# Gate column sums of the second layer as steps of the attention flow, and the last residual on one engine

## The chip, the cores and the metric

One core of a Trainium2 chip runs the whole program. The metric is device time in microseconds; 793.57 us is the median of three runs of the kernel before (793.48 to 795.55). The engines are named as in the profile: PE (matrix products), DVE (vector), ACT (scalar), POOL (GpSimd), and SP, which only issues transfers. Each engine works through its own list of instructions in a fixed order; where an instruction waits, all behind it on that engine wait too.

## The reference

Two layers work on 512 latent tokens and 256 context tokens of width 1024. Layer 0 is differential attention, layer 1 grouped-query attention with 8 query heads and 2 key heads. Both have the same frame:

```
shift, scale, gate = split(silu(c) @ ada_w[i] + ada_b[i])
h = rms_norm(x, pre_g[i]) * (1 + scale) + shift
y = (attention(h) * silu(z)) @ w_out[i]
x = x + gate * rms_norm(y, post_g[i])
```

The change concerns two pieces of layer 1: the gate, a row of 1024 numbers made from silu(c) and a 1024 x 1024 part of `ada_w[1]`, and the last line, which adds the gated, normalised product to the residual x. In layer 1 only the latent tokens are kept.

## The kernel before

**Numbers and stages.** All products are done in three matmuls on split operands (a high part, and the rest), `mm3`, whose recorder has line 155. The order of the stages is: layer 0 up to about 445 us of the trace; its output product, the residual and the transposed input of layer 1; the keys and values of layer 1 (K and V); then layer 1's attention from about 575 us, with the remaining query projections (`q_proj`) and gate-path projections (`z1_proj`) as filling; last the output product, tile by tile of 128 tokens, and the store of `out`.

**The planner.** The attention of a layer is traced by `flow` (L366). It holds streams of `Step`s, each with a cost in microseconds of a planner's clock and a due time: its own `at`, and lags behind other steps. The step that is due first is traced; while none is due, `piece` (L331) traces one more piece of the projections in `fillq` and moves the clock on by its cost. In layer 1 a score unit (S_, L1527) is a quarter of a head's tokens: six score matmuls, a maximum on DVE (L1537), an exponential on ACT (L1543), a reciprocal on DVE (L1544), the scaling of the weights on POOL (L1545, recorded in L233). There are 32, `TS/2` = 4.52 us of clock apart at the soonest, and each at least `SLAG1` behind the one two before. T_ steps transpose the weights and split them into `ah` (ACT, L1561) and `al` (DVE, L1562); M_ steps multiply them with the values (L167), at least `LM[layer]` behind their transposes. X_ steps transpose queries, Y_ steps finish the gate. `LM[0]` is the lag in layer 0 and `LM[1]` that in layer 1.

**Order on the engines.** Steps marked hot are traced at a raised priority (`HOT0`, `HOT1`, one number for each stream); the builder then places each engine's instructions by priority, as soon as what they need is there. An instruction may so stand well ahead of its place in the code: the first two gate loads are issued at 554.9 us, while values are still being projected. `tc.issue_after(ins)` ties instructions behind `ins` on the same engine.

**The gate.** `gate1_part` (L1585) is called eight times right after `q_proj(0)`, before any other filling. Each call loads 512 KB of `ada_w[1]` from SP into one of two buffers `gw`, and DVE multiplies each of its two 128 x 512 halves with a column of silu(c) and adds it to `gate1` (L1596 for the first of a half, else L1598). `gate1_finish` (L1600) sums `gate1` over the partitions with two matmuls, adds `ada_b` and multiplies by `post_g`; its two calls come at units 10 and 13 (`GFIN`).

**A bank and its readers.** The four PSUM banks of projections and transposes are handed round. A bank of `q_proj` is free again when ACT has squared it (L1408) and DVE has formed the two rope products `ta` (L1397) and `tb` (L1399, two instructions; `tb` has one buffer, which POOL empties in L1402).

**The end.** For each token tile the last columns of the output product are squared and summed on ACT (L1672), gated on DVE (L1688), and with the reciprocal root r (for the last tile L424 and L425 on ACT) the residual is formed in two pieces of 512 on DVE (L1703). For the last tile they are three: 512 columns on DVE, 256 as a scaling on ACT (L1700) and a sum on POOL (L1701), and 256 on DVE. Each piece is stored, the middle one from ACT, the others from SP (L1704).

Of the kernel before, what the change touches and what calls it, by code (L numbers as in the profile page):

```python
# [9 lines left out]
F32 = mybir.dt.float32  # L10
F32R = mybir.dt.float32r
AF = mybir.ActivationFunctionType
ALU = mybir.AluOpType
# [3 lines left out]
P = 128  # L17
# [16 lines left out]
ACD = 0.54  # L34
FILL1 = (('q', 1), ('z', 0), ('z', 2), ('q', 2), ('z', 1), ('q', 3), ('z', 4), ('z', 5), ('z', 3), ('z', 6), ('z', 7))
HOT0 = (4682, 2421, 950, 3759)
HOT1 = (1476, 3151, 2600, 3663, 2938)
WARM = 1817
AGB = 10
PRE = 16.26  # L40
# [13 lines left out]
LT = (1.27, 1.44)  # L54
AHEAD = 2
SLAG = (4.74, 1.08)
SLAG1 = 5.1
AT1 = 12.82
EGL = 'v'
EXS = 'pvvvvv'  # L60
# [15 lines left out]
EG1 = 'a'  # L76
EGA = "v"
RL = 3.57
LM = (4.78, 5.5)
AB = 3  # L80


# [5 lines left out]
def tile_backbone(  # L88
# [23 lines left out]
    nc = tc.nc  # L112
    uid = [0]

    def nm(s):
        uid[0] += 1
        return f"{s}_{uid[0]}"
# [8 lines left out]
    def small(n=1):  # L126
        return sm.tile([P, 8], F32, tag="sm", name=nm("sm"), bufs=24)[:, :n]
# [10 lines left out]
    def pj(n):  # L138
        i = lru.pop(0)
        o = banks[i][:, :n]  # L140
        held[id(o)] = (o, i)
        return o
# [62 lines left out]
    scol = con.tile([P, 2, KT], F32, name="scol")  # L205
# [29 lines left out]
    VP = {"v": nc.vector, "p": nc.gpsimd}  # L235
# [56 lines left out]
    def get_wout(layer, c, n):  # L292
        return [ws.get(k) for k in wout_keys(layer, c, n)]
# [18 lines left out]
    @contextmanager  # L312
    def onward(prev):
        if prev is None:
            yield
        else:
            with tc.issue_after(prev.ins), tc.high_priority(offset=20000):
                yield

    def hot(f, *args):  # L320
        with tc.high_priority(offset=HOT):
            f(*args)
# [8 lines left out]
    def piece():  # L331
        i = 0
        while i < min(len(fillq), AHEAD):
            try:
                cost = next(fillq[i])
            except StopIteration:
                fillq.pop(i)
                continue
            if cost is None:
                i += 1  # L340
                continue
            clock[0] += cost
            return True
        return False

    def drain(gen=None):
        while fillq and (gen is None or gen in fillq):
            ok_ = piece()
            assert ok_ or not fillq or (gen is not None and gen not in fillq)
# [16 lines left out]
    def flow(layer, streams):  # L366
        streams = [list(q) for q in streams]
        while any(streams):
            if layer == 0:
                rope_due()  # L370
            due, i = min((q[0].due(), i) for i, q in enumerate(streams) if q)
            if due > clock[0] and piece():
                continue
            assert due < 1e8
            step = streams[i].pop(0)
            clock[0] = max(clock[0], due)
            if step.hot:
                with tc.high_priority(offset=(HOT0, HOT1)[layer][i]):
                    step.f()
            else:  # L380
                step.f()
            clock[0] += step.cost
            step.t = clock[0]

    def chunk(layer, tstep, mstep, kts, after, ts, ms):
        for i, kt in enumerate(kts):
# [3 lines left out]
            if len(ms) >= AB:  # L390
                t.lag.append((ms[-AB], 0.0))
            m = Step(lambda kt=kt: mstep(kt), 0.65, [(t, LM[layer])])
            ts.append(t)
# [34 lines left out]
    def run(gen):  # L428
        for _ in gen:
            pass  # L430

    def out_proj(o, ghi, glo, w, m, n, lo=0, hi=KT):
        sl = slice(m * P, (m + 1) * P)
        per = 1024 // n
        for kt in range(lo, hi):
            wh, wl = w[kt // per]
            c = slice((kt % per) * n, (kt % per) * n + n)
            mm3(o, ghi[kt][:, sl], glo[kt][:, sl], wh[:, c], wl[:, c], kt == 0, kt == KT - 1)
            yield 3 * n / 2400.0
# [373 lines left out]
    with tc.tile_pool(name="t0", bufs=1) as t0:  # L813
# [39 lines left out]
        def rope_due():  # L853
            while ropeq and ropeq[0][0] <= clock[0]:
                ropeq.pop(0)[1]()

        def last_of(eng):
            return next(i for i in reversed(nc.cur_bb.bb.instructions) if i.engine == eng.engine)

        def qk_split(*args):  # L860
            with tc.high_priority(offset=WARM):
# [30 lines left out]
        def qr_tile():  # L892
            return t0.tile([P, T], F32, tag="qr", name=nm("qr"), bufs=4)
# [256 lines left out]
        for which, o in enumerate((oq, ok)):  # L1150
            r = qr_tile()
# [24 lines left out]
        S_, T_, M_, X_ = [], [], [], []  # L1176
# [101 lines left out]
    x1 = [h1p.tile([P, D], F32, name=f"x1_{t}", bufs=1) for t in range(NQ)]  # L1278
    gate1 = h1p.tile([P, D], F32, name="gate1")
# [98 lines left out]
    with tc.tile_pool(name="t1", bufs=1, side="right") as t1p:  # L1378
# [81 lines left out]
        t1q = ctx.enter_context(tc.tile_pool(name="t1q", bufs=1))  # L1460
# [121 lines left out]

            chunk(1, tstep, mstep, (0, 2, 4), [after], ts, ms)

        def gate1_part(half, k2):  # L1585
            acc = gate1[:, half * 512:half * 512 + 512]
            gw = t1q.tile([P, 1024], F32, tag="gw", name=nm("gw"), bufs=2)
            nc.sync.dma_start(
                gw.rearrange("p (k n) -> p k n", k=2),
                ada_w[1, k2 * 256:(k2 + 1) * 256, 2 * D + half * 512:2 * D + half * 512 + 512].rearrange("(k p) n -> p k n", p=P),  # L1590
            )
            for k in range(2):
                kt = k2 * 2 + k
                gs = gw[:, k * 512:(k + 1) * 512]
                if kt == 0:
                    VP[EGA].tensor_scalar(acc, gs, scol[:, 0, kt:kt + 1], None, ALU.mult)  # L1596
                else:
                    VP[EGA].scalar_tensor_tensor(acc, gs, scol[:, 0, kt:kt + 1], acc, ALU.mult, ALU.add)  # L1598

        def gate1_finish(half):  # L1600
            acc = gate1[:, half * 512:half * 512 + 512]
            o = pj(512)
            colsum(o, acc, [t1q.tile([P, 512], F32R, tag=t, name=nm("ac"), bufs=n) for t, n in (("za", 1), ("sz", 2))])
            b = wp.tile([P, 1024], F32, tag="raw", name=nm("raw"), bufs=2)
            sl = slice(half * 512, half * 512 + 512)
            nc.sync.dma_start(b[:, :512], ada_b[1, 2 * D + half * 512:2 * D + half * 512 + 512].partition_broadcast(P))
            nc.sync.dma_start(b[:, 512:], post_g[1, sl].partition_broadcast(P))
            nc.vector.tensor_tensor(acc, o, b[:, :512], ALU.add)
            close(o)
            nc.vector.tensor_tensor(acc, acc, b[:, 512:], ALU.mult)  # L1610
# [12 lines left out]

        add(q_proj(0))
        drain()
        for i in range(8):
            gate1_part(i // 4, i % 4)
        for kind, i in fill1:
            add({"q": q_proj, "z": z1_proj}[kind](i))
        S_, T_, M_, X_ = [], [], [], []  # L1630
# [15 lines left out]
        for h in range(KT):  # L1646
# [4 lines left out]
            for ch in range(2):  # L1651
                at, u = s1_units(h, (2 * ch, 2 * ch + 1))
                for i, st_ in enumerate(u):
                    st_.at = at_ + TS * (h * 2 + ch + i / 2)
                    st_.lag.append((qtr[h], 2.5))
                    if len(S_) >= 2:
                        st_.lag.append((S_[-2], SLAG1))
                    if len(T_) >= 6:
# [3 lines left out]
                    T_.append(Step(tail1, 0.0, [(M_[-1], 0.0), (u[-1], 0.0)]))  # L1662
                pv1_steps(h, at, ch, u[-1], T_, M_)
        Y_ = [Step(lambda i=i: gate1_finish(i), 0.9, [(S_[GFIN[i]], 0.0)], hot=False) for i in range(2)]
        flow(1, [S_, T_, M_, X_, Y_])
        drain()
        w_o = w_o[0]
        u, ss = {}, {}
# [5 lines left out]
        for qi, (c, n) in enumerate(OUTC1):  # L1674
            w = get_wout(1, c, n) if qi else w_o
            if qi == 0:
                for m in range(NQ):
                    run(out_proj(o_pre[m], ghi, glo, w, m, n, KT - 1, KT))
            for m in range(NQ):
                o = pj(n) if qi else o_pre[m]  # L1680
                if qi:
                    run(out_proj(o, ghi, glo, w, m, n))
                if qi == 0:
                    ss[m] = small(3)
                    u[m] = [t1p.tile([P, 512], F32, tag="g1", name=nm("u"), bufs=8) for _ in range(2)]
                ud = u[m][c // 512][:, c % 512:c % 512 + n]
                sumsq(ss[m][:, qi:qi + 1], o, n)
                nc.vector.tensor_tensor(ud, o, gate1[:, c:c + n], ALU.mult)  # L1688
                if qi:
                    close(o)  # L1690
                if qi == 1:
                    part_sum(ss[m])
                if qi == 2:
                    end = m == NQ - 1
                    r = (rstd_last if end else rstd_sum)(ss[m][:, 2:3], ss[m][:, 0:1])
                    for i, (a, b) in enumerate(((512, 1024), (0, 256), (256, 512)) if end else ((512, 1024), (0, 512))):
                        j = a // 512
                        uj = u[m][j][:, a - j * 512:b - j * 512]
                        if end and i == 1:
                            nc.scalar.activation(uj, uj, AF.Copy, scale=r)  # L1700
                            nc.gpsimd.tensor_tensor(uj, uj, x1[m][:, a:b], ALU.add)  # L1701
                        else:
                            nc.vector.scalar_tensor_tensor(uj, uj, r, x1[m][:, a:b], ALU.mult, ALU.add)  # L1703
                        (nc.scalar if i == 1 else nc.sync).dma_start(out[m * P:(m + 1) * P, a:b], uj)  # L1704
            ws.release(*wout_keys(1, c, n))

# [102 lines left out]
```

## Time and profile before

| | us |
|---|---|
| median of the runs | 793.57 |
| the profiled execution | 794.91 |
| its span, first to last instruction | 793.1 |
| PE busy | 775.7 (98%) |
| DVE busy | 526.5 (66%) |
| ACT busy | 455.1 (57%) |
| POOL busy | 326.5 (41%) |
| last matmul ends | 787.0 |

The times within the trace are those of the one profiled execution, in us from the first instruction; around its span lie 1.8 us more. A row of the timeline has the start, the duration, the engine, the line of the kernel, the operation, what is written and read, and in brackets the engine's idle time before it and what ended it. The granted clock of PE was 0.998.

### The profile page before, as it was taken

To read this page: it belongs to the slowest core of one execution; us is meant where nothing else is said; L and a number is where in the kernel's file an instruction comes from. 1 tells how busy PE (TensorE), PEld (TensorE's weight loads), DVE (VectorE), ACT (ScalarE), POOL (GpSimd) and SP (SyncE) were. 2 spreads that over 40 slices of the span, in tenths; PEclk is the share of its full clock that TensorE was granted. 3 is DMA by queue.
4 is the path that set the end of the run, shared out by engine and by line. 5 is a ranking of instruction groups with operands and counts; after the bars stand their busy time and mean duration, and the time that the engine had idled before them with its cause. 6 is when DMAs were issued, how large, how long until landed. Compare 5 with 4: busy or idle time off the path is not lost.

```text
span 793.1 us, 14232 instructions
## 1 busy us (share of the span) xinstructions
PE 775.7 (98%) x5446; PEld 698.8 (88%) x5446; DVE 526.5 (66%) x939; ACT 455.1 (57%) x995; POOL 326.5 (41%) x435
## 2 busy tenths in 40 slices
PE   8999999999999999999999999999989999999996
PEld 6688888888888898888979998899979999989986
DVE  4656676886877557866478743666876787565634
ACT  5546555674565644765468742665446576676632
POOL 1111376753446453363434412574535454334102
PEclk9999999999999999999999999999999999999999
DMA  9934211231323222323321051041740212010102
GB/s 341 381 103 140 80 54 41 67 105 68 134 80 107 93 81 67 120 93 107 127 74 54 28 212 55 1 140 54 249 149 30 54 54 81 27 54 28 54 27 107
DMA packets 35092, 77.77 MB, mean 98 GB/s; under 512 B 3408, under 2 KB 10064, under 8 KB 35024
## 3 DMA queue, kind: packets, MB, share of 16 engines
q1 hardware_dynamic: 31168, 71.05, 26.6%
q10 hardware_dynamic: 3856, 5.81, 2.1%
q8 instruction: 43, 0.70, 0.4%
q14 instruction: 25, 0.20, 0.1%
HBM read 70.56 MB, written 2.10 MB: 92 GB/s over the span
## 4 chain that ended last, share of the span: by engine, by line
PE 86%; DMA 4%; DVE 4%; POOL 2%; ACT 2%; issue 2%; DVEq 0%; SPq 0%; ACTq 0%; POOLq 0%
PE bk L155 54%; PE sc L155 10%; PE bk L167 9%; PE sc L994 5%; PE bk L1558 3%; PE bk L1059 3%; DMA gw<-in_ada_w 2%; PE bk L832 1%; DMA xnt<-in_xlT 1%; PE sc L1023 1%; POOL wlo L219 1%; PE bk L403 1%; DMA raw<-in_b_w 1%; POOL qk L219 1%; DVE wlo L219 1%
## 5 line engine op out<-in xcount | busy, mean ns | idle before, releaser
L155 PE MATMUL bk<-whi,h 128*128 128x256 f32 (+1 forms) x1184 | 244.2, 299 | 2.7 <-DVE tb L1399 2.7
L155 PE MATMUL bk<-h,whi 128*128 128x512 f32 (+2 forms) x864 | 228.5, 347 | 0.0
L155 PEld LDWEIGHTS bk<-whi,h 128*128 128x128 f32 x1184 | 191.8, 191 | 12.9 <-issue 3.4
L155 PE MATMUL bk<-wlo,h 128*128 128x256 f32 (+1 forms) x592 | 175.5, 299 | 0.0
L155 PEld LDWEIGHTS bk<-h,whi 128*128 128x128 f32 x864 | 150.4, 189 | 17.0 <-issue 2.7
L155 PE MATMUL bk<-h,wlo 128*128 128x512 f32 (+2 forms) x432 | 149.4, 346 | 0.0
L233 POOL TENSOR_SCALAR p<-p,sm 128x768 f32<-128x768 f32 (+1 forms) x80 | 68.2, 855 | 172.1 <-DVE sm L1005 81.1
L155 PEld LDWEIGHTS bk<-wlo,h 128*128 128x128 f32 x592 | 112.5, 191 | 3.8 <-issue 0.7
L219 DVE TENSOR_TENSOR wlo<-raw,whi 128x1024 fp32r<-128x1024 f32 (+1 forms) x66 | 82.5, 1254 | 26.7 <-ACT whi L225 26.3
L155 PEld LDWEIGHTS bk<-h,wlo 128*128 128x128 f32 x432 | 81.5, 189 | 8.0 <-issue 1.3
L1002 ACT ACTIVATE p<-sc,sm 128x768 f32<-128x768 f32 (+1 forms) x68 | 59.7, 878 | 47.9 <-DVE sm L999 47.8
L225 ACT CAST whi<-raw 128x1024 fp32r<-128x1024 f32 x64 | 67.1, 1051 | 29.6 <-PE bk L155 24.2
L999 DVE TENSOR_REDUCE sm<-sc 128x1 f32<-128x768 f32 (+1 forms) x68 | 60.5, 916 | 19.1 <-PE sc L994 18.9
L219 POOL TENSOR_TENSOR sz<-sz,za 128x192 f32<-128x192 f32 (+1 forms) x48 | 34.0, 730 | 70.4 <-ACT za L199 70.3
L1562 DVE TENSOR_TENSOR al<-bk,ah 128x512 fp32r<-128x512 f32 x48 | 32.1, 686 | 21.3 <-ACT ah L1561 18.2
L994 PE MATMUL sc<-qk,qk 64*128 64x384 f32 (+1 forms) x396 | 43.9, 351 | 0.7 <-ACT p L1002 0.7
L1063 DVE TENSOR_TENSOR al<-bk,ah 128x512 fp32r<-128x512 f32 x56 | 37.4, 682 | 7.4 <-ACT ah L1062 7.4
L1010 DVE SCALAR_TENSOR_TENSOR p<-p,sm,p 128x768 f32<-128x768 f32 (+1 forms) x34 | 39.4, 1158 | 4.1 <-POOL p L233 1.1
L1062 ACT CAST ah<-bk 128x512 fp32r<-128x512 f32 x56 | 31.6, 590 | 16.0 <-PE bk L1059 15.0
L1543 ACT ACTIVATE p<-sc,sm,qrs 128x768 f32<-128x768 f32 x32 | 31.9, 998 | 15.0 <-DVE sm L1540 11.6
L994 PEld LDWEIGHTS sc<-qk,qk 64*128 64x128 f32 x396 | 32.8, 184 | 7.8 <-issue 2.5
L1059 PE MATMUL bk<-ident,p 128*128 128x128 f32 x224 | 34.9, 275 | 2.0 <-DVE al L1063 1.5
(242 smaller groups left out, 1491.7 us busy)
## 6 DMA issues: line engine op xcount, KB each, us to landing
raw<-in_a_w SPq DMA_DIRECT2D x28, 512.0 KB, 3.5
araw<-in_ada_w SPq DMA_DIRECT2D x12, 1024.0 KB, 5.2
raw<-in_b_w SPq DMA_DIRECT2D x20, 512.0 KB, 3.6
ag<-in_ada SPq DMA_DIRECT2D x16, 512.0 KB, 7.8
raw<-in_w_out SPq DMA_DIRECT2D x16, 512.0 KB, 3.6
sw<-qr ACTq DMA_DIRECT2D x32, 128.0 KB, 2.1
gw<-in_ada_w SPq DMA_DIRECT2D x8, 512.0 KB, 4.3
xnt<-in_xlT SPq DMA_DIRECT2D x4, 512.0 KB, 5.5
```

What stands on the lines that cost most here:

```text
L155: i = nc.tensor.matmul(o, a, b, start=start, stop=stop)
L167: nc.tensor.matmul(o, v[:, kt + e, c], a[:, e * 256:e * 256 + 256], start=first and i == 0, stop=last and i == 5)
L219: eng.tensor_tensor(dst[:, i:i + n], a[:, i:i + n], b[:, i:i + n], op)
L225: nc.scalar.copy(hi, r)
L233: (nc.vector if eng == "v" else nc.gpsimd).tensor_scalar(dst, src, s_, 1.0, ALU.mult, ALU.mult)
L994: prev = nc.tensor.matmul(sc[m][:, j if nk == T else m, :w], a[r, tok], b[r, c], start=i == 0, stop=i == 2)
L999: nc.vector.tensor_reduce(mx, scv, AX.XY if nk == T else AX.X, ALU.max, negate=True)
L1002: nc.scalar.activation(pv_, scv, AF.Exp, bias=mx, accum_out=l[:, m:m + 1])
L1010: nc.vector.scalar_tensor_tensor(ps_[0], pt, r, ps_[0], ALU.mult, ALU.add)
L1059: nc.tensor.transpose(tr[:, e * 256 + i * P:e * 256 + (i + 1) * P], a[:, j * P:(j + 1) * P], ident)
L1063: nc.vector.tensor_tensor(al, tr, f32(ah), ALU.subtract)
L1562: nc.vector.tensor_tensor(al, tr, f32(ah), ALU.subtract)
```

## The change

The eight calls of `gate1_part` ahead of the filling are gone. A new stream Z_ of steps, not hot and of cost 0, takes their place in `flow`: load k comes behind score unit k+1, and the two sums of load k behind unit k+3, tied by `issue_after` behind the last DVE instruction traced so far. In the last token tile all three pieces of the residual are formed on DVE. Three constants differ: `SLAG1` goes from 5.1 to 4.72, `LM[0]` from 4.78 to 4.64, and `HOT1` has a sixth entry for the sixth stream.

```
-HOT1 = (1476, 3151, 2600, 3663, 2938)
+HOT1 = (1476, 3151, 2600, 3663, 2938, 0)
-SLAG1 = 5.1
+SLAG1 = 4.72
-LM = (4.78, 5.5)
+LM = (4.64, 5.5)
...
+    def last_of(eng):
+        return next(i for i in reversed(nc.cur_bb.bb.instructions) if i.engine == eng.engine)
...
-        def gate1_part(half, k2):
-            acc = gate1[:, half * 512:half * 512 + 512]
-            gw = t1q.tile([P, 1024], F32, tag="gw", name=nm("gw"), bufs=2)
+        gws = {}
+
+        def gate1_load(half, k2):
+            gw = gws[half, k2] = t1q.tile([P, 1024], F32, tag="gw", name=nm("gw"), bufs=2)
             nc.sync.dma_start(
                 gw.rearrange("p (k n) -> p k n", k=2),
...
+        def gate1_part(half, k2):
+            acc = gate1[:, half * 512:half * 512 + 512]
+            gw = gws.pop((half, k2))
+            with tc.issue_after(last_of(nc.vector)):
+                for k in range(2):
+                    kt = k2 * 2 + k
+                    gs = gw[:, k * 512:(k + 1) * 512]
+                    if kt == 0:
+                        nc.vector.tensor_scalar(acc, gs, scol[:, 0, kt:kt + 1], None, ALU.mult)
+                    else:
+                        nc.vector.scalar_tensor_tensor(acc, gs, scol[:, 0, kt:kt + 1], acc, ALU.mult, ALU.add)
...
         add(q_proj(0))
         drain()
-        for i in range(8):
-            gate1_part(i // 4, i % 4)
...
-        flow(1, [S_, T_, M_, X_, Y_])
+        Z_ = []
+        for i in range(8):
+            if i >= 0:
+                Z_.append(Step(lambda i=i: gate1_load(i // 4, i % 4), 0.0, [(S_[1 + i], 0.0)], hot=False))
+            if i:
+                Z_.append(Step(lambda i=i: gate1_part((i - 1) // 4, (i - 1) % 4), 0.0, [(S_[1 + i + 1], 0.0)], hot=False))
+        Z_.append(Step(lambda: gate1_part(1, 3), 0.0, [(S_[1 + 9], 0.0)], hot=False))
+        flow(1, [S_, T_, M_, X_, Z_, Y_])
...
-                        if end and i == 1:
-                            nc.scalar.activation(uj, uj, AF.Copy, scale=r)
-                            nc.gpsimd.tensor_tensor(uj, uj, x1[m][:, a:b], ALU.add)
-                        else:
-                            nc.vector.scalar_tensor_tensor(uj, uj, r, x1[m][:, a:b], ALU.mult, ALU.add)
+                        nc.vector.scalar_tensor_tensor(uj, uj, r, x1[m][:, a:b], ALU.mult, ALU.add)
```

More of the change, by code (lines that the diff above doesn't have):

```diff
@@ L855, in rope_due @@
                 ropeq.pop(0)[1]()
-        def last_of(eng):
-            return next(i for i in reversed(nc.cur_bb.bb.instructions) if i.engine == eng.engine)
         def qk_split(*args):
@@ L1591, in gate1_part @@
             )
[L1592 to L1596, printed above, removed]
-                else:
-                    VP[EGA].scalar_tensor_tensor(acc, gs, scol[:, 0, kt:kt + 1], acc, ALU.mult, ALU.add)
+        def gate1_part(half, k2):
[9 more added lines that the diff above has]
+                        nc.vector.scalar_tensor_tensor(acc, gs, scol[:, 0, kt:kt + 1], acc, ALU.mult, ALU.add)
         def gate1_finish(half):
@@ L1698, in tile_backbone @@
                         uj = u[m][j][:, a - j * 512:b - j * 512]
-                        if end and i == 1:
[L1700 to L1703, printed above, removed]
+                        nc.vector.scalar_tensor_tensor(uj, uj, r, x1[m][:, a:b], ALU.mult, ALU.add)
                         (nc.scalar if i == 1 else nc.sync).dma_start(out[m * P:(m + 1) * P, a:b], uj)
```

## The prediction

> **What bounds the kernel now.** I read the page's busy shares first, then what PE waited for from 60 us to the end of its work.
>
> ```profile
> span 793.1 us, 14232 instructions
> PE 775.7 (98%) x5446; PEld 698.8 (88%) x5446; DVE 526.5 (66%) x939; ACT 455.1 (57%) x995; POOL 326.5 (41%) x435
> ```
>
> PE is busy 98% of the span. The edit takes no matmul away and adds none, so it can move the time in two ways only: through PE's idle stretches, and through what follows the last matmul. The view of waits on PE lists every such stretch after 60 us (us in total, times, longest):
>
> ```profile
> PE bk L155 <- DVE tb L1399: 2.7, 1, 2.7
> PE bk L1059 <- DVE al L1063: 1.5, 2, 1.0
> PE sc L994 <- ACT p L1002: 0.7, 1, 0.7
> PE sc L1350 <- POOL xn L1342: 0.6, 1, 0.6
> PE bk L832 <- DVE al L1063: 0.6, 1, 0.6
> PE bk L1059 <- DVE p L1010: 0.5, 1, 0.5
> PE sc L155 <- ACT p L1543: 0.4, 1, 0.4
> PE bk L167 <- DVE al L1063: 0.2, 1, 0.2
> ```
>
> One wait of 2.7 us stands out; the other seven lines sum to 4.5 us, and only the one of 0.4 (L1543) lies in the second layer's attention. The timeline around the long one shows its cause:
>
> ```profile
> 572.34 8.96 SPq L1588 DMA_DIRECT2D gw<-in_ada_w  x3
> 575.51 0.29 DVE L1399 TENSOR_TENSOR tb<-bk,ropeb 128x128 f32<-128x128 f32 x1 [0.59 <-POOL q L1402]
> 576.47 0.34 PE L155 MATMUL sc<-kl,qh 128*128 128x384 f32 x1
> 578.52 0.75 DVE L1598 SCALAR_TENSOR_TENSOR gate<-gw,scol,gate 128x512 f32<-128x512 f32 x1 [2.73 <-DMA gw<-in_ada_w]
> 579.19 0.28 DVE L1399 TENSOR_TENSOR tb<-bk,ropeb 128x128 f32<-128x128 f32 x1
> 579.53 0.39 PE L155 MATMUL bk<-whi,h 128*128 128x256 f32 x1 [2.72 <-DVE tb L1399]
> ```
>
> The rotary product tb at 579.19 is what empties a projection bank, and PE's next projection needs that bank. On DVE it stood behind a gate sum (L1598) whose weights had not landed. DVE idled 2.73 us for the transfer, and PE idled 2.72 us behind it. This is the wait that the edit reaches.
>
> **The gate sums leave this place.** Their price, from the view of the tile gw and the groups on DVE between 555 and 590 us:
>
> ```profile
> L1598 DVE SCALAR_TENSOR_TENSOR gate<-gw,scol,gate 128x512 f32<-128x512 f32 x14 | 10.9, 782 | 4.8 <-DMA gw<-in_ada_w 4.7
> L1596 DVE TENSOR_SCALAR gate<-gw,scol 128x512 f32<-128x512 f32 x2 | 1.4, 724 | 1.0 <-DMA gw<-in_ada_w 1.0
> L1598 DVE SCALAR_TENSOR_TENSOR gate<-gw,scol,gate x14: 733/743/1110, 559.3 to 586.3; 128x512 f32<-128x512 f32 x14
> DMA to landing us min/median/max: 3.7/4.3/6.2
> ```
>
> In the new order the sum of piece k is traced after score unit k+3 and tied behind the last DVE instruction that then stands. So it can no longer stand ahead of that q projection's rope, and the 2.72 us go. What is late next at this point? The first tb ended at 575.80, so the second could end by about 576.1; PE finishes its score matmul at 576.47 + 0.34 = 576.81. The bank is free 0.7 us before PE asks, so I take the whole 2.72.
>
> **What the sums meet in the new place.** They add 14 x 0.782 + 2 x 0.724 = 12.4 us of DVE, in pairs of 1.55 us, between units 3 and 10. The reductions of units 0 to 31 run from 585.4 to 731.6 (a row of L1537, below), so units 3 to 10 lie at about 600 to 635 us. The windows view (busy PE, PEld, DVE, ACT, POOL):
>
> ```profile
> L1537 DVE TENSOR_REDUCE sm<-sc x32: 940/951/959, 585.4 to 731.6; 128x1 f32<-128x768 f32 x32
> 560.00:590.00 30.00, 27.28 (x198) 25.91 (x198) 24.66 (x50) 11.71 (x37) 15.84 (x22) 1.00 0.60 191
> 590.00:640.00 50.00, 50.00 (x347) 47.70 (x346) 33.45 (x67) 34.27 (x75) 23.35 (x31) 1.00 0.18 54
> ```
>
> DVE goes from 33.45 to 33.45 + 12.4 = 45.85 of 50 us, 92%. It fits, but the idle time that absorbs a late input shrinks from 16.5 to 4.2 us. A sum cannot be stopped once begun, so a split of the softmax weights (al, L1562), which PE needs for its next product, can come up to a pair, 1.55 us, later. Behind a sum that waits stand the next unit's reduction, such splits and the rope products; PE waits for all three. The nearest approach of a split to its use in this stretch:
>
> ```profile
> 634.89 0.68 DVE L1562 TENSOR_TENSOR al<-bk,ah 128x512 fp32r<-128x512 f32 x1
> 637.18 0.40 PE L167 MATMUL bk<-al,vh 128*128 128x256 f32 x2
> 637.79 0.68 DVE L1562 TENSOR_TENSOR al<-bk,ah 128x512 fp32r<-128x512 f32 x1
> 639.43 0.40 PE L167 MATMUL bk<-al,vh 128*128 128x256 f32 x2
> ```
>
> The first al lies 1.61 us ahead of its use, the second 0.96. A pair in front of the second costs PE 1.55 - 0.96 = 0.6 us; the earlier splits of the stretch lie further ahead. The bound is 0 to 1.2 us (two such hits); a gain is excluded, since PE is busy 50.00 of 50 there. I take 0, for the first margin covers a whole pair. The column sums that read the gate come at units 10 and 13, three units or more behind the last sum of their half: 14 us of cover.
>
> **The loads.** Eight issues on SP move, with two buffers: load k+2 waits until sum k has read its buffer, and sum k+2 comes two units later. Thirty-one unit steps between 585.4 and 731.6 make 4.7 us each, 9.4 for two; the slowest landing above is 6.2. So 3 us of cover remain, and DVE stops waiting for them (5.8 us of idle in the two rows above). SP runs in order, so a weight load behind a waiting gate load waits too. The nearest:
>
> ```profile
> 601.47 0.33 SPq L223 DMA_DIRECT2D raw<-in_b_w  x1
> 616.58 1.05 ACT L225 CAST whi<-raw 128x1024 fp32r<-128x1024 f32 x1 [0.29 <-PE bk L155]
> 624.89 0.33 SPq L223 DMA_DIRECT2D raw<-in_b_w  x1
> 635.13 1.04 ACT L225 CAST whi<-raw 128x1024 fp32r<-128x1024 f32 x1
> ```
>
> Issue to first use is 15 and 10 us, of which landing takes 6.2 at most: at least 4 us of cover, which costs nothing unless a sum is later than that. In the old place 512 KB pieces also took DMA time beside the projections' weights (share 0.60 against 0.18); that relief hides nothing PE waits for.
>
> **The tail.** The last tile's middle quarter leaves ACT and POOL:
>
> ```profile
> 787.63 0.42 DVE L1688 TENSOR_TENSOR u<-bk,gate 128x256 f32<-128x256 f32 x1 [0.26 <-ACT jk L1672]
> 788.41 0.51 ACT L1700 ACTIVATE u<-u,sm 128x256 f32<-128x256 f32 x1
> 788.41 1.61 DVE L1703 SCALAR_TENSOR_TENSOR u<-u,sm,x 128x512 f32<-128x512 f32 x2 [0.35 <-ACT sm L425]
> 788.99 0.75 POOL L1701 TENSOR_TENSOR u<-u,x 128x256 f32<-128x256 f32 x1 [3.07 <-ACT u L1700]
> L1703 DVE SCALAR_TENSOR_TENSOR u<-u,sm,x x8: 744/752/946, 782.0 to 789.1; 128x512 f32<-128x512 f32 x7, 128x256 f32<-128x256 f32 x1
> ```
>
> DVE now ends at 788.41 + 1.61 = 790.02, and its last piece, 256 wide, took 0.946, longer than a 512-wide one (0.75). That piece ended 0.28 us after POOL's at 789.74. With POOL silent a quarter should take about what the 256-wide product L1688 took, 0.42: three pieces are 0.75 + 2 x 0.42 = 1.59 end to end, and less by two overlaps of 0.09 (the two pieces of 0.75 and 0.95 took 1.61 together), 1.41. Against 1.61 the gain is 0.02 to 0.2 us; I take 0.1. If a quarter took as long as before, 0.95, it would be a loss of up to 0.9. The stores follow as before, the last from SP behind DVE's end.
>
> [...]
>
> **The constants.** A sixth entry in HOT1 is for a stream that isn't hot: nothing. SLAG1 (5.1 to 4.72) lets a score unit follow the one two before sooner, in the planner's time; units are 4.7 us apart, so it binds only when the planner is behind. It could deepen the 0.4 us wait for the exponential (L1543): 0 to 0.4. LM's first number belongs to the first layer: there each product is planned 0.14 us sooner after its transposes. PE's order changes only where this lets a product pass a piece of projection, at most three matmuls. The first layer's waits in the list (all but the first, L1350 and L1543) sum to 3.5 us; a shift may remove some or add as many. Bounds -1.75 to +1.75 (half of them), value 0.
>
> **Sum.** The profiled execution took 794.91 (span 793.1 and 1.8 around it): 794.91 - 2.72 - 0.1 = 792.1. The median of the runs, 793.57, is 1.34 below the profiled one, so the forecast is 790.8, 0.35% faster. A measurement tells about 0.3%, 2.4 us, from no change, and 2.8 is just past that.
>
> **The rivals.** First: the stall goes and part of it comes back. DVE's 92% brings 1.2 us as bounded above, or the first layer's order loses up to 1.75. From 0.4 us back the result is within 0.3%: 791.2 to 793.6. For it speaks how thin 4.2 us of idle is; against it, margins of 1.6 us and more nearly everywhere.
>
> Second, and slower than before: DVE overflows between 590 and 640. Each of the 16 sums would wait for a POOL instruction, the scaling of a unit's weights being the longest that is frequent:
>
> ```profile
> L233 POOL TENSOR_SCALAR p<-p,sm 128x768 f32<-128x768 f32 x32 | 29.2, 914 | 55.5 <-DVE sm L1544 39.0 <-DVE sm L1540 8.7 <-PE bk L1494 7.8
> ```
>
> Then a sum takes 0.78 + 0.91, DVE needs 33.45 + 12.4 + 16 x 0.91 = 60.4 of 50 us, the work behind runs 10.4 late, and PE, which has up to 1.6 us of margin at the end of the stretch, stands for 8.8: 790.8 + 8.8 = 799.6. It decides from 4.2 / 16 = 0.26 us of added wait per sum. Against it: beside a POOL that was busy 15.84 of 30 us the sums averaged 0.782 with a median of 0.743, and in the new stretch POOL is busy 23.35 of 50, a smaller share. [...]
>
> Third: the edit doesn't do what it says. The sums are only held behind what is traced before them, so a load could still be late with DVE standing at it: the old wait at a new place, 793.5. Two units between a buffer's release and its next use speak against it.
>
> **How the numbers follow.** Forecast case 0.54 (790.8; its own range 788.9 to 791.2); first rival 0.32 and third 0.07, both within 0.3%; second rival 0.07. The range's low end takes 2.2 us more, half of the 4.5 us of other waits: 788.6. The high end gives all 2.8 back: 793.6. Faster 0.54, same 0.39, slower 0.07.
>
> **What would show it.** Right: no wait of PE for tb of more than 0.7 us, no idle time of DVE in front of L1598's successors for gw, sums between 595 and 640, PE idle there under 0.5 us, an end of DVE's last piece about 1.5 us after ACT's reciprocal root. Wrong: rows of PE waiting for al, ql or tb between 595 and 645, sums above 1 us on average, or a first layer whose waits differ from 3.5 us by more than 1.

## The result and the profile after

| | before | after |
|---|---|---|
| median of 14 runs, us | 793.9 | 792.62 |
| lowest to highest | 793.48 to 796.34 | 792.21 to 793.01 |
| profiled execution | 794.91 | 792.77 |
| its span | 793.1 | 790.8 |

The ratio of the times is 0.9979, with a 95% interval of 0.9971 to 0.9987: a gain of 0.2%, clear of noise but under the 0.3% that the forecast needed for "faster". The means lie 1.7 us apart and the medians 1.3; the difference comes from three executions of the kernel before at 795.55 to 796.34. In the later rounds such lengths went with a lower mean granted clock of PE, 0.994 to 0.997 against 0.997 to 0.999 (below). The forecast of 790.8 was 1.8 us too low; 792.62 lies within its range.

The view of waits on PE after 60 us, for the kernel after (in total, times, longest):

```profile
PE bk L1059 <- DVE gate L1133: 1.1, 1, 1.1
PE sc L1350 <- POOL xn L1342: 0.7, 1, 0.7
PE sc L994 <- ACT p L1002: 0.7, 1, 0.7
PE bk L1059 <- DVE al L1063: 0.6, 1, 0.6
PE bk L835 <- DVE al L1063: 0.6, 1, 0.6
PE sc L155 <- ACT p L1543: 0.4, 1, 0.4
PE bk L167 <- DVE al L1063: 0.4, 1, 0.4
```

The wait of 2.7 us for tb is gone, and no new one stands in the second layer: only L1350 and L1543 belong to it, and both were there before. The tile gw, and the windows 540 to 590 and 590 to 640 (busy PE, PEld, DVE, ACT, POOL, the clock, the DMA share):

```profile
L1604 DVE SCALAR_TENSOR_TENSOR gate<-gw,scol,gate x14: 725/742/1291, 597.6 to 638.5; 128x512 f32<-128x512 f32 x14
L1602 DVE TENSOR_SCALAR gate<-gw,scol x2: 460/465/470, 597.0 to 618.9; 128x512 f32<-128x512 f32 x2
DMA to landing us min/median/max: 3.8/4.1/5.0
```

```profile
540.00:590.00 50.00, 50.00 (x382) 48.57 (x381) 27.27 (x60) 24.18 (x69) 23.51 (x34) 1.00 0.32 106
590.00:640.00 50.00, 50.00 (x360) 48.20 (x359) 44.71 (x83) 33.85 (x73) 26.56 (x30) 1.00 0.39 118
```

The sums run from 597 to 639 us, no idle time of DVE stands in front of them, DVE is busy 44.71 of 50 us (45.85 were forecast), and PE has no idle time in either window. At the end, DVE's row of the last tile:

```profile
786.15 1.54 DVE L1710 SCALAR_TENSOR_TENSOR u<-u,sm,x 128x512 f32<-128x512 f32 x3 [0.35 <-ACT sm L428]
L1710 DVE SCALAR_TENSOR_TENSOR u<-u,sm,x x9: 479/746/752, 779.7 to 787.2; 128x512 f32<-128x512 f32 x7, 128x256 f32<-128x256 f32 x2
```

Three pieces took 1.54 us, against 1.61 for two pieces before, and a quarter took 0.48, against 0.95 beside POOL.

So far every step holds. To see why less came out, PE's work can be cut in two: from the first score matmul of the first layer (L994) to the first transpose for the second (L1350), and from there to the last matmul. Of the kernel before, and of the kernel after:

```profile
74.75:499.24 424.49, 421.01 (x2988) 373.74 (x2988) 290.45 (x482) 247.05 (x531) 191.47 (x238) 1.00 0.26 87
499.24:787.03 287.79, 284.01 (x1981) 267.55 (x1979) 187.88 (x353) 166.37 (x383) 122.89 (x177) 1.00 0.23 73
```

```profile
74.81:499.83 425.02, 421.58 (x2988) 373.21 (x2987) 287.59 (x482) 247.45 (x531) 187.54 (x238) 1.00 0.27 87
499.83:784.77 284.94, 283.78 (x1981) 267.78 (x1979) 186.71 (x353) 166.84 (x383) 125.97 (x177) 1.00 0.23 73
```

The second layer is 287.79 - 284.94 = 2.85 us shorter, close to the forecast 2.72. The first is 425.02 - 424.49 = 0.53 us longer, with as many matmuls: PE's busy time, 421.01 to 421.58, and not its waits, grew. Only LM[0] touches the first layer.

### The profile page after: what moved, and what is told of

Same layout as the page of the kernel before. It is cut to its first block, busy times and chain, and to the rows that moved or that the text cites. A ratio compares the mean times of both kernels' runs of the same rounds, so it can differ in the third digit from the quotient of the medians.

```text
span 790.8 us, 14236 instructions
## 1 busy us (share of the span) xinstructions
PE 776.8 (98%) x5446; PEld 699.2 (88%) x5446; DVE 522.4 (66%) x940; ACT 455.4 (58%) x994; POOL 324.9 (41%) x434
## 4 chain that ended last, share of the span: by engine, by line
PE 89%; DVE 3%; ACT 3%; DMA 2%; POOL 1%; issue 1%; SPq 0%; DVEq 0%; ACTq 0%; POOLq 0%
PE bk L155 56%; PE sc L155 10%; PE bk L167 9%; PE sc L994 5%; PE bk L1059 3%; PE bk L1558 3%; PE bk L835 1%; DMA xnt<-in_xlT 1%; PE sc L1023 1%; POOL wlo L219 1%; DMA raw<-in_b_w 1%; DVE al L1063 1%; PE bk L406 1%; PE bk L407 1%; ACT p L1033 0%
## 5 line engine op out<-in xcount | busy, mean ns | idle before, releaser
L233 POOL TENSOR_SCALAR p<-p,sm 128x768 f32<-128x768 f32 (+1 forms) x80 | 71.7, 899 | 163.1 <-DVE sm L1005 63.9
L219 DVE TENSOR_TENSOR wlo<-raw,whi 128x1024 fp32r<-128x1024 f32 (+1 forms) x66 | 80.7, 1226 | 34.4 <-ACT whi L225 34.3
L219 POOL TENSOR_TENSOR sz<-sz,za 128x192 f32<-128x192 f32 (+1 forms) x48 | 35.1, 752 | 65.8 <-ACT za L199 65.7
L994 PE MATMUL sc<-qk,qk 64*128 64x384 f32 (+1 forms) x396 | 43.8, 351 | 0.7 <-ACT p L1002 0.7
L1062 ACT CAST ah<-bk 128x512 fp32r<-128x512 f32 x56 | 31.6, 589 | 19.0 <-PE bk L1059 16.6
L1543 ACT ACTIVATE p<-sc,sm,qrs 128x768 f32<-128x768 f32 x32 | 31.9, 996 | 15.1 <-DVE sm L1540 8.9
L994 PEld LDWEIGHTS sc<-qk,qk 64*128 64x128 f32 x396 | 32.8, 184 | 7.7 <-issue 3.4
L1561 ACT CAST ah<-bk 128x512 fp32r<-128x512 f32 x48 | 26.9, 588 | 17.9 <-PE bk L1558 14.6
```

The costliest lines, as they stand in the source:

```text
L219: eng.tensor_tensor(dst[:, i:i + n], a[:, i:i + n], b[:, i:i + n], op)
L233: (nc.vector if eng == "v" else nc.gpsimd).tensor_scalar(dst, src, s_, 1.0, ALU.mult, ALU.mult)
L994: prev = nc.tensor.matmul(sc[m][:, j if nk == T else m, :w], a[r, tok], b[r, c], start=i == 0, stop=i == 2)
L1543: nc.scalar.activation(pt.rearrange("p (j n) -> p j n", j=2), scv, AF.Exp, scale=sr, bias=nmx, accum_out=l)
```

## The experiments

The main theory is that the late gate load made PE wait and that LM[0] costs time (A). Against it stand: that the wait is always 2.7 us and the moved sums give some 1 us back (B); that the first layer's loss is chance (C); that the order on SP is what counts (D), or the place of the sums (E). A theory on the clock came up on the way, with its own rival, that the wait's length alone sets the time (F).

The runs came in three later rounds. The median of the kernel before was 795.33 us in the first of them (its second profile, the move alone, the old constants, the move without the tie), 794.31 in the second (LM[0] = 4.64, three buffers, one buffer, every sum twice) and 793.82 in the third (the rest). Each ratio is against its own round, so ratios of different rounds are compared with care. The executions of the kernel before that stayed under 795 us, all at a granted clock of 0.997 or more, have medians of 794.1, 793.9 and 793.7 there; gains in us are measured from these.

**The kernel before, profiled again.** No edit.

> The kernel before, unchanged, profiled a second time. Theory A: the wait of PE behind the gate sum is the rest of a transfer, so its length differs from execution to execution, and the whole execution is as much longer: PE's wait for tb (L1399) is some other length than 2.7 us, between 1.0 and 2.7, and the time less that wait is again 794.91 - 2.72 = 792.2, within 0.4. Rival B: the wait is always about 2.7, and the moved sums give some 1 us back in the new kernel: the wait is 2.7 again, at a time near the median of 793.9, so that the time less the wait is 791.2.

```profile
PE bk L155 <- DVE tb L1399: 2.2, 1, 2.2
```

794.05 us, with a wait of 2.2: 791.85 without it, within the 0.4 of 792.2 that A allows. B falls. In the first profile the wait of 2.72 us stood behind DVE's 2.73 for a gate load, the rest of a transfer, and that was a long one.

**The move alone.** The whole change with `LM = (4.78, 5.5)`, `SLAG1 = 5.1` and the old tail.

> The kernel before with the new steps for the gate alone: old constants, old tail. Theory A: no wait of PE for tb; the first layer is that of before, its last score matmul ending at 437.5 (438.1 after the whole change), so this is 0.5 us faster than the whole change in the first layer and 0.1 slower in the tail: 0.4 us below the whole change's 792.6, ratio to before about 0.9975. Rival C: the first layer's 0.6 us is chance of the execution and the constants cost nothing: 0.1 us slower than the whole change, ratio 0.998 to 0.9985, last score matmul of the first layer anywhere between 437.5 and 438.1.

792.03 us, ratio 0.9964 (0.9951 to 0.9977): 2.1 us below 794.1, and 0.6 below the whole change, as A has it. The two parts of PE's work:

```profile
74.49:498.59 424.10, 421.01 (x2987) 373.67 (x2987) 289.77 (x482) 247.13 (x531) 192.23 (x238) 1.00 0.26 87
498.59:783.79 285.20, 283.81 (x1981) 267.77 (x1979) 187.31 (x353) 166.80 (x383) 125.28 (x177) 1.00 0.23 73
```

The first layer is that of before, 421.01 of busy time to the hundredth.

**The whole change with the old constants.**

```
-LM = (4.64, 5.5)
+LM = (4.78, 5.5)
-SLAG1 = 4.72
+SLAG1 = 5.1
```

> The changed kernel with the two old constants, LM[0] = 4.78 and SLAG1 = 5.1 (the new steps and the new tail stay). Theory A: the first layer as before (last score matmul ends at 437.5), 0.5 to 0.6 us faster than the whole change, about 792.1; the tail from the last matmul to the end of the span 6.0 us (6.1 before). Rival C: no difference to the whole change, 792.6.

791.85 us, ratio 0.9961 (0.9946 to 0.9975); from the last matmul to the end of the span 6.0 us, against 6.1 for the move alone (789.89 - 783.79). C falls here.

**The whole change with LM[0] = 4.78.** Here SLAG1 stays at 4.72; the order of the instructions on PE, DVE and SP is the same as with 5.1.

> The changed kernel with LM[0] = 4.78 alone (SLAG1 stays at 4.72; no engine's list differs from that with both old constants). Theory A: first score matmul to first L1350 in 424.0 to 424.5 us, no PE wait for tb, one group of times within 1 us around 791.9, ratio 0.995 to 0.9975, below the whole change's 0.9979. Rival C: 792.6 and ratio 0.998.

791.5 us (791.37 to 792.02), ratio 0.9967 (0.9954 to 0.9979). No PE wait for tb, and

```profile
74.72:498.99 424.27, 420.99 (x2987) 373.84 (x2987) 290.87 (x482) 246.88 (x531) 191.12 (x238) 1.00 0.26 87
```

These two kernels, the same in order, are the best of this study: below both the kernel before and the whole change by their medians.

**LM[0] = 4.64 in the kernel before.**

> The kernel before with LM[0] = 4.64 alone. Theory A (the constant costs time in the first layer, as PE's own time and not as waits): from the first score matmul to the first transpose of the second layer's input (L1350) 425.0 us or more, where the kernels with 4.78 had 424.1 to 424.5; PE's wait for tb stays at 2 us or more; 0.6 to 0.9 us slower than before, ratio 1.0005 to 1.0015. Rival C (chance): 424.1 to 424.5 and ratio 1.000.

795.76 us, ratio 1.0015 (1.0000 to 1.0029). It ran 425.26 us from the first score matmul (74.86) to the first L1350 (500.12): the constant alone makes the first layer as long as in the whole change. But the second layer, too, was longer in this execution (797.27 us), and the windows show why (the clock is the last column but two):

```profile
577.00:580.80 3.80, 1.74 (x13) 1.41 (x12) 1.88 (x4) 1.03 (x5) 0.91 (x2) 1.00 0.47 171
580.80:584.20 3.40, 3.40 (x15) 3.40 (x15) 3.40 (x8) 1.05 (x1) 2.32 (x3) 0.50 0.47 127
584.20:590.00 5.80, 5.80 (x32) 5.07 (x32) 5.74 (x10) 2.65 (x7) 2.08 (x3) 1.00 0.41 116
```

Right behind the wait for tb, PE ran 3.4 us at half its clock: 15 matmuls, where 3.4 us of the row below hold 19. The twelve executions fall into two groups: six at 794.43 to 794.87 us with a mean clock of 0.998 or more, six at 796.65 to 797.32 with 0.996 or 0.997.

**Two more profiles of it**, for the clock.

> The kernel before with LM[0] = 4.64 again, one more profile. Its 12 timed executions fell into two groups, 794.43 to 794.87 and 796.65 to 797.32, and the profiled one (797.27) had PE's clock at one half from 580.8 to 584.2 us, right behind a PE wait of 2.1. Clock theory: the wait lets the granted clock drop in some executions, and that alone parts the groups: a time below 795.2 shows no half clock between 570 and 600, a time above 796.3 shows 3.4 us or a multiple of it. Rival F (the groups come from the length of the wait): no half clock in either, and a time above 796.3 goes with a wait above 4 us.

> As lm464_b, a third profile. Clock theory: again the half clock and the upper group go together, and the lower group goes with a full clock behind a wait of about the same length, 2 to 2.8 us. Rival F: no half clock, the wait's length follows the time.

797.31 us with a half clock, and 794.96 us without one. The wait on PE, of the one and of the other:

```profile
PE bk L155 <- DVE tb L1399: 2.9, 1, 2.9
```

```profile
PE bk L155 <- DVE tb L1399: 1.8, 1, 1.8
```

The windows of the one with the half clock, which lay from 579.8 to 583.2:

```profile
577.00:580.80 3.80, 0.89 (x5) 0.56 (x4) 1.49 (x4) 0.60 (x3) 0.39 (x1) 0.87 0.42 153
580.80:584.20 3.40, 3.40 (x20) 3.40 (x20) 3.40 (x8) 0.91 (x1) 2.67 (x4) 0.64 0.38 89
```

The two profiles with a half clock took 797.27 and 797.31 us, behind waits of 2.1 and 2.9; without one stood 794.96 us and a wait of 1.8 here, and waits of 2.2 and 2.7 in the kernel before with its own constant. The length of the wait has a part: of the 2.35 us between these two executions, 2.9 - 1.8 = 1.1 are the wait itself. But F is refuted, for 797.31 came with a half clock and with a wait of 2.9, not above 4. The 1.8 lies just below the 2 to 2.8 that the clock theory named, but 2.7 us in the kernel before left the clock whole. The clock parts the groups, and not only here. Of the 54 executions of the kernel before in these rounds, 33 took 792.89 to 794.88 us at a mean clock of 0.997 to 0.999, and 21 took 795.28 to 797.75 at 0.994 to 0.997. One stretch of 3.4 us at half clock lowers the mean over 795 us by 0.002. Of the 65 executions of the kernels whose profile has no wait for tb (the whole change included, every sum twice not), none was below 0.997.

**A third buffer for the gate loads, in the kernel before.**

```
-gw = t1q.tile([P, 1024], F32, tag="gw", name=nm("gw"), bufs=2)
+gw = t1q.tile([P, 1024], F32, tag="gw", name=nm("gw"), bufs=3)
...
-return sm.tile([P, 8], F32, tag="sm", name=nm("sm"), bufs=24)[:, :n]
+return sm.tile([P, 8], F32, tag="sm", name=nm("sm"), bufs=16)[:, :n]
```

> The kernel before with three buffers for the gate's weights in place of two (and 16 small scratch buffers in place of 24, to make room, which alone leaves every engine's order as it was); sums and loads stay among the projections. Theory A (only the late load matters, not the place of the sums): each load goes out a pair of sums sooner, DVE's idle time for gw falls from 5.2-5.7 to under 1.5 us, PE's wait for tb to under 0.3, and the time is that of the move alone, ratio 0.9955 to 0.997. Rival E (the sums crowd the rope products and the weights' splits where they stand): PE keeps a wait of 1 us or more for DVE there, ratio above 0.998.

793.06 us, ratio 0.9984 (0.9975 to 0.9994): 0.9 us below 793.9, less than half of the move's 2.1. The wait for tb is gone and DVE's idle time for gw is 2.0 us. PE's waits between 545 and 760 us are now these:

```profile
PE sc L155 <- ACT p L1543: 0.5, 1, 0.5
PE bk L1558 <- POOL qrs L1411: 0.4, 1, 0.4
PE bk L1558 <- ACT g L1575: 0.3, 1, 0.3
```

The second layer took 286.2 us from the first L1350 (498.76) to the last matmul (784.94), 1.0 more than with the move. So A is right on the wait for tb but not on the time, and E is right on the time but not on the wait of 1 us or more that it named. That the 16 sums among the rope products have a price of their own is likely; the two new waits are 0.7 of it, and the rest isn't settled.

**One buffer.**

```
-gw = t1q.tile([P, 1024], F32, tag="gw", name=nm("gw"), bufs=2)
+gw = t1q.tile([P, 1024], F32, tag="gw", name=nm("gw"), bufs=1)
```

> The kernel before with one buffer for the gate's weights. Theory A: each load starts only when the sums before it are done, so DVE stands for most of a landing (4 us) several times, 10 us or more in all, wherever the builder put the sums; PE's waits behind DVE between 555 and 600 us grow from 2.7 to 4 us or more, ratio 1.002 or above. Rival D (the order of issues on SP decides, not the landing): no more than 2.7 us of PE waits, ratio 1.000.

795.26 us, ratio 1.0006 (0.9993 to 1.0019). DVE stood 11.6 us for gw, twice as long as before, and yet none of it became a wait for tb. PE's waits in the same stretch:

```profile
PE sc L155 <- ACT p L1543: 1.3, 2, 0.8
PE bk L1558 <- DVE al L1562: 1.1, 1, 1.1
PE sc L155 <- DVE ql L1498: 0.3, 1, 0.3
```

A's numbers for this kernel failed; D's came (2.7 us of PE waits, ratio 1.000), though the run doesn't show that SP's order is the reason. DVE's idle time is no measure of PE's loss: the builder placed the sums anew, from 559 to 603 us, and the one that waited 2.17 us at 577.49 stands behind both instructions of tb.

**The move without the tie.**

```
-            with tc.issue_after(last_of(nc.vector)):
+            if True:
```

> The changed kernel with the new steps, but the sums not tied behind the last DVE instruction. The builder then puts sums and loads back among the second layer's query projection, nearly where they stood before. Theory A: the tie is what does it: DVE stands at a load again and PE waits 1.0 to 2.7 us behind a rope product, time 0.5 above before less 0.1 for the tail, ratio 0.999 to 1.001. Rival D: the loads' new places in SP's order (three of them ahead of two weight loads) already take the wait away: no wait of PE between 555 and 595 us, ratio 0.998 as the whole change.

793.19 us, ratio 0.9979 (0.9970 to 0.9989). The sums went back to 560 to 586 us and DVE stood 4.4 us for gw, as A said; but PE's waits between 545 and 760 us were these two alone:

```profile
PE sc L155 <- ACT p L1543: 0.4, 1, 0.4
PE bk L155 <- ACT jk L1408: 0.2, 1, 0.2
```

A failed here as well. D's forecast came but for 0.2 us, and its reason did not: the issues on SP stand in the same order as in the kernel before (two gate loads, two weights, three, two, three). Of the kernel before (its next row, 572.34, stands in the prediction), and of this one:

```profile
560.12 7.72 SPq L1588 DMA_DIRECT2D gw<-in_ada_w  x3
569.15 2.14 SPq L223 DMA_DIRECT2D raw<-in_b_w  x2
```

```profile
560.96 7.75 SPq L1589 DMA_DIRECT2D gw<-in_ada_w  x3
570.02 2.14 SPq L223 DMA_DIRECT2D raw<-in_b_w  x2
573.21 7.40 SPq L1589 DMA_DIRECT2D gw<-in_ada_w  x3
```

What differs is DVE's order at one place. In the kernel before, the sum that waits stands between the two instructions of tb (575.51 and 579.19 in the prediction's rows). Here it stands behind both:

```profile
576.38 0.49 DVE L1399 TENSOR_TENSOR tb<-bk,ropeb 128x128 f32<-128x128 f32 x2 [0.59 <-POOL q L1402]
578.20 0.75 DVE L1604 SCALAR_TENSOR_TENSOR gate<-gw,scol,gate 128x512 f32<-128x512 f32 x1 [1.33 <-DMA gw<-in_ada_w]
```

DVE stood 1.33 us, and PE had its bank. The tie keeps the sums out of this stretch, so it doesn't leave the matter to such an order. The eleven runs spread over 1.55 us (792.57 to 794.12), the whole change over 0.8; why these spread isn't settled.

**Every sum twice**, the whole change with the old constants and this behind each sum; the output is not touched:

```
+                    for _ in range(1):
+                        scr = t1q.tile([P, 512], F32, tag="scr", name=nm("scr"), bufs=1)
+                        nc.vector.scalar_tensor_tensor(scr, gs, scol[:, 0, kt:kt + 1], gs, ALU.mult, ALU.add)
```

> The changed kernel with the two old constants, and a second instruction behind each of the 16 gate sums, of the same form and size, into a scratch tile: DVE has 16 x 0.8 to 0.9 = 13 to 14 us more between 595 and 640, where it was busy 44.7 of 50. Overflow theory (second rival of the prediction): 58 of 50 us, the softmax splits come late and PE waits 3 to 9 us behind DVE between 595 and 660; ratio 1.000 to 1.008. Slack theory: the sums are last in priority and slide to later gaps, PE's waits in 595 to 660 sum to under 1 us, ratio 0.996 to 0.998.

> The kernel with every gate sum followed by a second one into a scratch tile, for its profile (time 801.5, against 791.9 without). Overflow theory: PE's waits between 595 and 660 us sum to 4 us or more, all behind DVE's splits, rope products or maxima, and DVE is busy 49 of 50 us between 595 and 645. Clock theory adds that half clock rows of 3.4 us follow some of these waits. Slack theory (another cause): PE's waits there sum to under 2 us, and the 9.6 us lie elsewhere.

801.55 us, ratio 1.0089 (1.0068 to 1.0109), 9.7 us more than with single sums. The first profile took 1090.38 us at a mean clock of 0.646, unlike any other here, so the rows are those of the second (802.0 us), PE's waits from 545 to 760 us and some windows:

```profile
PE bk L155 <- DVE al L1562: 2.7, 1, 2.7
PE bk L1558 <- DVE al L1562: 1.4, 1, 1.4
PE bk L1558 <- ACT sz L1517: 0.8, 1, 0.8
PE sc L155 <- ACT p L1543: 0.4, 1, 0.4
PE bk L167 <- DVE al L1562: 0.3, 1, 0.3
```

```profile
610.00:620.00 10.00, 9.54 (x74) 8.97 (x73) 10.00 (x17) 6.28 (x13) 4.46 (x6) 1.00 0.45 130
620.00:630.00 10.00, 7.32 (x22) 5.61 (x21) 10.00 (x18) 2.91 (x8) 6.19 (x7) 0.66 0.46 135
622.00:628.80 6.80, 5.83 (x14) 4.57 (x15) 6.80 (x16) 2.33 (x7) 4.44 (x5) 0.50 0.48 158
640.00:650.00 10.00, 7.66 (x56) 6.74 (x55) 10.00 (x19) 7.28 (x14) 5.04 (x4) 1.00 0.37 116
```

DVE is full in these stretches, and PE waits for al: 2.7 + 1.4 + 0.3 us behind DVE. From the last microsecond of the wait of 2.7 on, the clock was at a half for 6.8 us; two executions at a mean clock of 0.998 took 801.4 and 801.55 us, so the half clock isn't what makes the time. This is the overflow of the second rival, at twice the load; at the load of the change it doesn't set in. That a sum waits for POOL is the rival's other part, which this run doesn't test.

## Why the forecast was right and wrong

**The wait removed: right.** The sums left, PE's next work was there in time, and the second layer became 2.85 us shorter in the profiled executions. That the move alone has 1 - 0.9964 = 0.36%, beside the 0.35% forecast for the whole, is luck: the kernel before ran at 795.33 in that round, and 792.03 is 1.2 us above the forecast time.

**Its size: mis-sized.** "I take the whole 2.72": that was one execution's. In the others with the sums at the old place the wait was 2.2, 2.1, 2.9 and 1.8. The sum was made against the profiled execution, which stood 1.34 above the median of its runs, and the full 2.72 was then carried to that median. The kernel after is only 0.15 above its own, since it has no such wait. This is 1.34 - 0.15 = 1.2 of the 1.8 us by which the forecast was too low; most of the rest is the first layer, below. On the other side, some executions of the old order lose more than the wait, by the half clock: of the 2.35 us between two of them (797.31 and 794.96) the wait is 1.1.

**The new place: right.** "I take 0": PE has no wait between 590 and 640, so the 1.2 us of the first rival did not come. The time fell to this rival all the same (791.2 to 793.6), by its other arm, the order of the first layer.

**The loads: right.** No DVE idle time for gw, landings of 3.8 to 5.0 us, and no PE wait for a weight.

**The tail: right.** 0.1 us was forecast; from the last matmul to the span's end it went from 793.13 - 787.03 = 6.10 to 790.77 - 784.77 = 6.00. The other profiles agree: 6.09 to 6.10 with the old tail, 6.00 to 6.02 with the new.

**The constants: wrong.** "Bounds -1.75 to +1.75 (half of them), value 0" for LM[0]. It costs 0.7 to 1.0 us in the first layer between kernels that differ in it alone: eight executions with 4.78 (the kernel before twice, the two buffer kernels, the move alone, the three of the change with the old LM[0]) took 424.1 to 424.6 us there, the five with 4.64 (the whole change, the one without the tie, and three of the kernel before with that constant) 425.0 to 425.4. The bounds held this, but they were built from waits. What grew is mostly PE's own time, 420.9 to 421.0 against 421.6 to 421.8, with the same number of matmuls in another order; not more changes of kind, since in either order the trace's matmuls change 105 times between the full array, 64 rows and 32 columns. What in the order costs this stays open. SLAG1 did nothing that the runs show, within the forecast's 0 to 0.4. Against the executions of the kernel before under 795 us (793.9 in the median among the runs of the first table, too) the change gains 2.2 to 2.3 us with the old LM[0] (791.5 and 791.85), and 1.3 with the new one (792.62).

**The second rival: some sums ran longer beside POOL, but by far less.** It charged each sum 0.91 us, the author's estimate that every sum waits for a whole POOL instruction, and needed 0.26. No run shows that term: the sums averaged 0.896 us in the new place, against 0.782, so 0.11 each (last section).

**The third rival: refuted for this kernel.** No DVE idle time for gw is left.

## What to carry to other kernels

When one engine waits for another that waits for a load, look at what is queued behind the waiting instruction: the loss is set by that, and not by how long the engine stands (11.6 us on DVE cost PE less than 3; one wait of 2.7 cost 2.7 ahead of tb, one of 1.33 behind it nothing). Carry a stall to a median only after a second profile, since the rest of a transfer differs from run to run (the wait for tb was 1.8 to 2.9 us). Time each constant alone: one number with no part in the main idea took back about 0.9 of 2.2 us.

## What the runs showed of the hardware

**A half clock behind some PE waits.** Waits of 2.1, 2.9 and 2.7 us (LM[0] = 4.64, first and second profile; every sum twice, second) went with 3.4, 3.4 and 6.8 us at a clock of 0.5. Waits of 2.7, 2.2 and 1.8 us (the kernel before, first and second profile; LM[0] = 4.64, third) did not. The length of the wait alone doesn't part them, since 2.7 stands on both sides. What does isn't shown: no run varied the wait on purpose.

**POOL's scaling took longer beside DVE's sums.** The scaling of the weights on POOL in the stretch 590 to 640, before and after:

```profile
L233 POOL TENSOR_SCALAR p<-p,sm 128x768 f32<-128x768 f32 x12 | 11.0, 914 | 14.1 <-DVE sm L1544 12.4 <-DVE sm L1540 1.6
```

```profile
L233 POOL TENSOR_SCALAR p<-p,sm 128x768 f32<-128x768 f32 x11 | 13.6, 1236 | 16.0 <-DVE sm L1544 8.6 <-PE bk L406 3.7 <-DVE sm L1540 3.6
```

The sums themselves, after, from 590 to 642 us:

```profile
L1604 DVE SCALAR_TENSOR_TENSOR gate<-gw,scol,gate 128x512 f32<-128x512 f32 x14 | 12.6, 896 | 0.1
```

The same instruction on POOL went from 0.91 to 1.24 us on average. Of the eleven, the seven that overlap a gate sum took 0.99 to 1.34, two that overlap DVE's L198 and L219 took 1.28 and 1.98, and the two that overlap none of these 0.91. PE had no wait from it in this stretch (50.00 of 50 us busy). Of the sums, four of 14 took 1.28 to 1.29, each beside POOL, and the others 0.73 to 0.79.
